# A two-layer decoder trunk on one core: where the conv taps stand among the attention score groups, and the order of the first weight's pieces

## The chip, the cores and the metric

The kernel runs on one core of a Trainium2 chip. The engines that matter are TensorE (PE in the profile, its weight loads PEld), VectorE (DVE), ScalarE (ACT), GpSimd (POOL) and SyncE (SP), which issues most DMAs. The metric is the time of one execution in device microseconds; lower is better. The time given for a kernel is the median of several runs.

## The reference

A trunk of two layers works on 512 tokens of width 1024 in float32. Cut to what matters here:

```python
for l in range(DEPTH):                                    # 2 layers
    h = x + 0.5 * swiglu(rms_norm(x, ffn1_norm[l]), w1, w3, w2)      # width 2816
    n = rms_norm(h, mix_norm[l])
    u_conv, q, k, v, q_mem = jnp.split(n @ w_in[l], splits, axis=-1)
    y_conv = conv_module(u_conv, ...)     # GLU, causal depthwise conv of 31 taps, 384 channels, LayerNorm, swish
    y_swa  = sliding_window_attention(...)  # 6 q heads, 2 kv heads, window 128, learned sinks
    y_mem  = memory_attention(...)        # 4 heads over 256 memory tokens
    h = h + jnp.concatenate([y_conv, y_swa, y_mem], -1) @ w_out[l]
    h = h + 0.5 * swiglu(rms_norm(h, ffn2_norm[l]), w1b, w3b, w2b)
    x = rms_norm(h, final_norm[l])
```

Each depthwise tap multiplies 384 channels of a shifted sequence by one weight per channel and adds it to a running sum. The attention subtracts the maximum of each row of scores (with the sink, in the windowed kind) before the exponential.

## The kernel before, in words

**Data and matmuls.** Activations lie with the channels on the 128 partitions and the 512 tokens along the free axis. A float32 product is made of three matmuls of a reduced float format (`mm3`, L176 to L178): high by high, high by low, low by high. So each weight and each operand is split into a high and a low part. The split is a ScalarE copy (the high part) and a VectorE subtraction (the low part, L145 and L146), or, where VectorE is to be spared, two ScalarE copies and a GpSimd DMA that adds the weight from memory once more (`split_by_dma`, L150 to L152). Operands are split by `split_scaled` (L155, L156).

**A layer.** `ffn` runs the first feed-forward block in quarters of its 22 column tiles. The gate tiles from the fifth on come in pairs by a scheme with seven products for eight (`up_pair`). `mixer` then runs the steps that the string ORDER lists: conv projections (`c`), queries (`q`) and their transposes (`Q`), values (`v`) and theirs (`V`), the first two score groups (`g`), the attention (`a`), the conv taps (`t`) and the swish with its LayerNorm (`s`). At the end the output projection's conv rows are added, and the second feed-forward block follows.

**Score groups.** `attention` walks through ten groups of (block, head pair). `begin(n)` puts the scores of group n into PSUM (`scored`, L763 and L769), VectorE takes their maxima (L773 or L788) and a bias (L774, or L789 and L790), ScalarE the exponentials (`powers`, L800), TensorE transposes them (`turned`, L810), ScalarE copies them (L812), TensorE multiplies by the values (`weighted`, L821), VectorE divides (`scaled`, L830 to L835), and `attended` transposes and splits the result (L844). Group n + 2 is begun while group n is worked on. The ScalarE exponential of the sink term (L829) needs a GpSimd sum (L791). The copies of the output weights' columns 0 to 3 (`out_weights`) stand in front of the loop and ahead of groups 3 and 5.

**Taps.** Three channel tiles of 31 taps make 93 VectorE operations a layer: one of L932 for each channel tile, and 30 of L939, each of which needs the one before it on the same channel tile. The first EARLY = 49 are free to start once their input is there. The other 44 are queued behind the biases of the ten groups, as many behind each as LATER says, with what is left over behind the last. In the program they come behind all of the attention.

**Swish.** GpSimd adds the three channel tiles (L945, L946), a matmul with ones gives the mean (L950), VectorE subtracts it (L953), ScalarE squares, and after the reciprocal root a spread over the partitions (`spread`, `kept`) gives the factor RL. Output rows of the attention parts (`out_rows`) are laid between these steps on TensorE.

**What sets the order.** The scheduler of the language orders each engine's instructions by a simulated timeline: the instruction that comes first in the program goes first among those that are ready. `tc.issue_after(x)` binds the block's instructions on x's engine to come behind x in that engine's order, and `queued()` does this with the last TensorE instruction. Every engine works its own list in order.

**Start.** SyncE loads the gains, then half of the first w1 tile, a chunk of x, half of the first w3 tile, and the other chunks of x with the second halves in the middle (L110 to L120).

Of the kernel before, what the change touches and what calls it, by code (L numbers as in the profile page):

```python
# [18 lines left out]
P = 128  # L19
# [45 lines left out]
def trunk(ctx: ExitStack, tc: tile.TileContext, xT, memT, pos, w1a, w3a, w2a, w1b, w3b, w2b,  # L65
# [44 lines left out]
    nc.sync.dma_start(gn, gains)  # L110
# [50 lines left out]
    def weights(src, cols, on, own=None):  # L161
        hi, lo = own or pair()
        if first:
            raw = first.pop(0)
            for c in halves:
                split(hi[:, c], lo[:, c], raw[:, c], V)
            return hi, lo
# [58 lines left out]
    class Stat:  # L226
# [5 lines left out]
        def square(self, out, src, scale):  # L232
            if self.on:
                self.on.tensor_tensor(out=out, in0=src, in1=src, op=ALU.mult)
            else:
                A.activation(out, src, AF.Square, scale=scale)
# [104 lines left out]
    def up_pair(l, w13, f, M):  # L341
# [26 lines left out]
        def add(out, a, b):  # L368
            V.tensor_tensor(out=out, in0=a, in1=b, op=ALU.add)  # L369
# [15 lines left out]
        for i in range(2):  # L385
# [4 lines left out]
            add(to[i][:, :, x1], zv[i].rearrange("p (n t) -> p n t", n=2), part[i][:, x0].unsqueeze(1).to_broadcast([P, 2, QT]))  # L390
# [14 lines left out]
    def ffn(l, w13, w2, x, sums, factors, last, at_product, aside=None):  # L405
# [138 lines left out]

    def head_scale(ps, col, n, out=None):

        sq = tm("hsq", "sq", 2)[:, 0 : n * HD]
        A.activation(sq, ps, AF.Square, scale=col)
# [74 lines left out]
    def mixer(l, x, st, last):  # L623
# [113 lines left out]

        def value_columns(t):
# [12 lines left out]
        sinks, nsinks = by_half(sink), by_half(nsink[:, l, :])  # L751

        def scored(kind, pairs):
# [17 lines left out]
            if not masked:  # L771
                for i in range(2):
                    V.tensor_reduce(out=nmr[:, b, i], in_=pp[i], axis=AX.X, op=ALU.max)  # L773
                biased[len(biased)] = V.scalar_tensor_tensor(out=nmr[:, b], in0=nmr[:, b], scalar=-1.0, in1=by_half(rm[:, b, :]),  # L774
                                                             op0=ALU.mult, op1=ALU.mult)
# [11 lines left out]
            for i in range(2):  # L787
                V.tensor_reduce(out=each(nmw, i), in_=pp[i], axis=AX.X, op=ALU.max)  # L788
            V.scalar_tensor_tensor(out=at_(nmw), in0=at_(nmw), scalar=-1.0, in1=rr, op0=ALU.mult, op1=ALU.mult)  # L789
            biased[len(biased)] = V.tensor_tensor(out=at_(nmw), in0=at_(nmw), in1=per(nsinks), op=ALU.min)  # L790
# [32 lines left out]
        def scaled(kind, b, po):  # L823
# [3 lines left out]
            if kind == "w":  # L827
                e = esw[:, b]
                A.activation(e, e, AF.Exp)  # L829
# [31 lines left out]
        def attention():  # L861
# [69 lines left out]
        def taps(c):  # L931
            V.tensor_scalar(out=cv[:, c, :], in0=ypad[:, c, 0:S], scalar1=conv_w[:, c, 0:1], scalar2=conv_b[:, c : c + 1],  # L932
                            op0=ALU.mult, op1=ALU.add)
            for j in range(1, TAPS):

                n = c * TAPS + j - EARLY
                group = sum(n >= sum(LATER[:g]) for g in range(1, len(LATER)))
                with tc.issue_after(biased[group].ins) if n >= 0 else nullcontext():
# [184 lines left out]
```

## Time and profile before

| | |
|---|---|
| median of 3 runs | 1791.62 us (1790.84 to 1792.38) |
| profiled execution | 1790.99 us |
| its span, first to last instruction | 1789.2 us |
| mean granted TensorE clock | 0.994 |
| HBM read, written | 249.40 MB, 2.10 MB |
| mean DMA rate | 142 GB/s |

The profile gives the busy time of each engine, and the trace every instruction with the idle time of its engine before it and what ended that time. Times are microseconds from the start of the span. The granted clock is the share of full speed that TensorE was given in a stretch. A row of the table of windows gives a stretch, its length, the busy time of each engine with the number of instructions, the granted clock, the share of the DMA engines and their rate. A row of the timeline gives start and length, engine, line, operation, what is written and read, and in brackets the idle time before it with what ended it.

### The profile page before, as it was taken

The numbers are of one execution on the slowest core, as the hardware profiler recorded it, in microseconds if no ns is written. First come the engines' busy times: TensorE is split into PE (matmuls) and PEld (weight loads), VectorE is DVE, ScalarE is ACT, GpSimd is POOL, SyncE is SP. The second block draws the span as 40 slices with busy tenths as digits, with TensorE's granted clock in tenths as the row PEclk, the third lists the DMA queues.
The fourth block names the chain that finished last, engine by engine and source line by source line (L and its number), as shares of the span: only waits on it lengthen the run. The fifth ranks groups of instructions, "written<-read, shape, count | busy, mean of one in ns | idle before, by whom it ended". The sixth has DMA issues, their size and how long they took to land.

```text
span 1789.2 us, 28081 instructions
## 1 busy us (share of the span) xinstructions
PE 1757.0 (98%) x11004; PEld 1581.5 (88%) x11004; DVE 1272.3 (71%) x1887; ACT 899.4 (50%) x1367; POOL 194.4 (11%) x217
## 2 busy tenths in 40 slices
PE   8999999999999999999999999999999999999997
PEld 6989999878788989898889898989787889998986
DVE  6969666589947857575678685756797567666755
ACT  6646444464765535353655453535455655453532
POOL 1001000034221000000010000000441210000000
PEclk9999999999999999999999999999999999999998
DMA  9456555183167547464656474643631966574622
GB/s 280 125 163 177 165 139 145 57 217 70 30 176 172 139 136 177 127 173 128 165 136 170 131 190 135 169 114 105 158 70 30 234 127 171 136 183 119 168 74 82
DMA packets 95892, 253.32 MB, mean 142 GB/s; under 512 B 9872, under 2 KB 14224, under 8 KB 95760
## 3 DMA queue, kind: packets, MB, share of 16 engines
q1 hardware_dynamic: 77040, 190.45, 34.9%
q0 software_dynamic: 18720, 61.09, 19.3%
q8 instruction: 86, 1.41, 0.3%
q14 instruction: 46, 0.38, 0.1%
HBM read 249.40 MB, written 2.10 MB: 141 GB/s over the span
## 4 chain that ended last, share of the span: by engine, by line
PE 81%; issue 6%; DVE 6%; DMA 4%; ACT 3%; POOL 0%; SPq 0%; POOLq 0%; DVEq 0%; ACTq 0%
PE mm L177 12%; PE mm L176 11%; PE mm L178 11%; PE po L176 8%; PE po L178 8%; PE po L177 8%; PE pt L176 6%; PE pt L177 6%; PE pt L178 6%; DVE there L939 2%; DMA glo<-in_wqk 1%; DMA raw<-in_wout 1%; DVE wlo L146 1%; PE cf L178 1%; PE cf L176 1%
## 5 line engine op out<-in xcount | busy, mean ns | idle before, releaser
L145 ACT ACTIVATE whi<-raw 128x1024 fp32r<-128x1024 f32 (+3 forms) x344 | 324.5, 945 | 440.5 <-PE mm L177 223.5
L146 DVE TENSOR_TENSOR wlo<-raw,whi 128x1024 fp32r<-128x1024 f32 (+3 forms) x344 | 372.0, 1083 | 133.9 <-ACT whi L145 132.6
L177 PE MATMUL mm<-glo,whi 128*128 128x512 f32 x752 | 293.3, 390 | 0.8 <-DVE glo L146 0.8
L176 PE MATMUL mm<-ghi,whi 128*128 128x512 f32 x752 | 293.3, 392 | 0.0
L178 PE MATMUL mm<-ghi,wlo 128*128 128x512 f32 x734 | 285.7, 389 | 0.9 <-DVE wlo L146 0.9
L177 PE MATMUL po<-ml,whi 128*128 128x256 f32 x864 | 244.5, 283 | 0.0
L178 PE MATMUL po<-mh,wlo 128*128 128x256 f32 x864 | 244.5, 283 | 0.0
L176 PE MATMUL po<-mh,whi 128*128 128x256 f32 x864 | 244.4, 283 | 0.0
L176 PE MATMUL pt<-xhi,whi 128*128 128x256 f32 x864 | 243.3, 283 | 0.6 <-DVE g L369 0.6
L178 PE MATMUL pt<-xhi,wlo 128*128 128x256 f32 x864 | 243.9, 283 | 0.0
L177 PE MATMUL pt<-xlo,whi 128*128 128x256 f32 x864 | 243.9, 283 | 0.0
L475 DVE SCALAR_TENSOR_TENSOR h<-mm,h 128x512 f32<-128x512 f32 x128 | 87.8, 689 | 133.3 <-PE mm L178 133.3
L177 PEld LDWEIGHTS mm<-glo,whi 128*128 128x128 f32 x752 | 141.3, 188 | 29.9 <-DVE glo L146 1.6
L176 PEld LDWEIGHTS mm<-ghi,whi 128*128 128x128 f32 x752 | 141.3, 188 | 29.4 <-DVE h L475 1.2
L176 PEld LDWEIGHTS pt<-xhi,whi 128*128 128x128 f32 x864 | 165.2, 192 | 1.7 <-DVE g L369 0.8
L177 PEld LDWEIGHTS pt<-xlo,whi 128*128 128x128 f32 x864 | 165.7, 192 | 0.8
L176 PEld LDWEIGHTS po<-mh,whi 128*128 128x128 f32 x864 | 165.8, 192 | 0.7
L177 PEld LDWEIGHTS po<-ml,whi 128*128 128x128 f32 x864 | 165.8, 192 | 0.6
L178 PEld LDWEIGHTS po<-mh,wlo 128*128 128x128 f32 x864 | 165.8, 192 | 0.0
L178 PEld LDWEIGHTS pt<-xhi,wlo 128*128 128x128 f32 x864 | 165.6, 192 | 0.0
L178 PEld LDWEIGHTS mm<-ghi,wlo 128*128 128x128 f32 x734 | 137.8, 188 | 30.2 <-DVE wlo L146 1.3
L939 DVE SCALAR_TENSOR_TENSOR there<-ypad,par,there 128x512 f32<-128x512 f32 x180 | 136.7, 770 | 1.6
(312 smaller groups left out, 3312.9 us busy)
## 6 DMA issues: line engine op xcount, KB each, us to landing
raw<-in_w2a SPq DMA_DIRECT2D x48, 384.0 KB, 3.5
raw<-in_w2b SPq DMA_DIRECT2D x48, 384.0 KB, 3.6
raw<-in_w1b SPq DMA_DIRECT2D x26, 512.0 KB, 3.7
raw<-in_w3b SPq DMA_DIRECT2D x26, 512.0 KB, 4.1
raw<-in_w1a SPq DMA_DIRECT2D x25, 512.0 KB, 3.7
raw<-in_w3a SPq DMA_DIRECT2D x25, 512.0 KB, 3.8
wsum<-in_w1a SPq DMA_DIRECT2D x18, 512.0 KB, 4.5
wsum<-in_w3a SPq DMA_DIRECT2D x18, 512.0 KB, 4.4
```

The source lines that it names most:

```text
L145: A.activation(hi, x, AF.Copy)
L146: on.tensor_tensor(out=lo, in0=x, in1=hi.bitcast(F32), op=ALU.subtract)
L176: T.matmul(ps, a[0], b[0], start=first, stop=False, **more)
L177: T.matmul(ps, a[0], b[1], start=False, stop=False, **more)
L178: tail[0] = T.matmul(ps, a[1], b[0], start=False, stop=last, **more)
L475: added = V.scalar_tensor_tensor(out=h[:, d, :], in0=ps, scalar=0.5, in1=h[:, d, :], op0=ALU.mult, op1=ALU.add)
L939: V.scalar_tensor_tensor(out=cv[:, c, :], in0=ypad[:, c, j : j + S], scalar=conv_w[:, c, j : j + 1], in1=cv[:, c, :], op0=ALU.mult, op1=AL ...
```

## The change

The change has seven parts.

1. Start: the first w1 tile comes in three pieces (256, 256 and 512 columns); the first quarter is loaded ahead of the gains, the second before the second chunk of x.
2. ORDER puts the values of block 2 (`v2`) ahead of `V1`, and the taps (`t`) ahead of the first score group. EARLY is 55. Each score group lays its own taps behind its bias, by the new LATER: 0, 8, 4, 3, 2, 1, 1, 1, 1 and 17. From the second group on, the maxima are queued behind the taps laid so far. The order of taps is: channel tile 0, 24 of tile 1, 17 of tile 2, then seven pairs that alternate between tiles 1 and 2, then the last seven of tile 2.
3. The exponential of the sink term goes behind the last exponential of its block. The output weights' columns 0 to 2 are split in the values of block 0, column 3 in those of block 2.
4. The second to fourth tile of the query weights are split behind the last square of the mixer's operand.
5. RL is copied by VectorE; the last pair of the conv output weights is copied behind the last swish.
6. The scaling of h by the block-output norm in layer 1 is done in two halves behind two successive pairs.
7. Helpers return the instructions that the others are bound to.

```diff
-ORDER = "c00 c01 q0 c10 q1 c11 Q0 q2 q3 Q1 c20 c21 Q2 v0 v1 V0 Q3 V1 g0 g1 v2 v3 a t0 t1 t2 s"
-EARLY = 49
-LATER = (1, 12, 5, 4, 3, 3, 3, 3, 3, 3)
+ORDER = "c00 c01 q0 c10 q1 c11 Q0 q2 q3 Q1 c20 c21 Q2 v0 v1 V0 Q3 v2 V1 t g0 g1 v3 a s"
+EARLY = 55
+LATER = (0, 8, 4, 3, 2, 1, 1, 1, 1, 17)
...
-    nc.sync.dma_start(gn, gains)
...
+    pieces = [slice(0, 256), slice(256, 512), slice(512, UNIT)]
     for k in range(KD):
-        if k % 4 == 0:
-            nc.sync.dma_start(first[0][:, halves[k // 4]], w1a[0, 0, :, halves[k // 4]])
+        if k in (0, 1, 4):
+            c = pieces[min(k, 2)]
+            nc.sync.dma_start(first[0][:, c], w1a[0, 0, :, c])
+        if not k:
+            nc.sync.dma_start(gn, gains)
...
-                    if f == PLAIN:
-                        with tc.issue_after(M.gated.ins):
-                            after()
+                    if f in (PLAIN, PLAIN + 2):
+                        with tc.issue_after((M.gated if f == PLAIN else M.turned).ins):
+                            after(f > PLAIN)
...
-                ww["q"] = [weights(wqk[l, i], 1024, G if i else V, spare()) for i in range(4)]
+                ww["q"] = []
+                for i in range(4):
+                    with tc.issue_after(operand.stats[0][0].done.ins) if i else nullcontext():
+                        ww["q"].append(weights(wqk[l, i], 1024, G if i else V, spare()))
...
+            for d in {0: (0, 1, 2), 2: (3,)}.get(t, ()):
+                with tc.issue_after((squared[-1] if d > 1 else keyed[2]).ins):
+                    out_weights(d)
...
+        to_do = [(c, j) for c in range(2) for j in range(TAPS)][:EARLY]
+        to_do += [(2, j) for j in range(TAPS - 14)]
+        for j in range(14):
+            to_do += [(1, j) for j in range(j + EARLY - TAPS, TAPS)][:1] if j + EARLY < 2 * TAPS else []
+            to_do.append((2, TAPS - 14 + j))
+        tapped = []
+
+        def taps(n=EARLY):
+            for c, j in [to_do.pop(0) for _ in range(n)]:
...
+        def between():
+            return tc.issue_after(tapped[-1].ins) if biased else nullcontext()
+
+        def taps_behind(small):
+            with tc.issue_after(small.ins):
+                taps(LATER[len(biased)])
+            biased[len(biased)] = small
...
-            for i in range(2):
-                V.tensor_reduce(out=each(nmw, i), in_=pp[i], axis=AX.X, op=ALU.max)
+            with between():
+                for i in range(2):
+                    V.tensor_reduce(out=each(nmw, i), in_=pp[i], axis=AX.X, op=ALU.max)
...
-                A.activation(e, e, AF.Exp)
+                with tc.issue_after(raised[kind, b, CC - 1].ins):
+                    A.activation(e, e, AF.Exp)
...
-            for d in range(2):
-                with tc.issue_after(keyed[2].ins):
-                    out_weights(d)
...
-                if n in (3, 5):
-                    with tc.issue_after(raised[GROUPS[n - 1][0], *GROUPS[n - 1][-1]].ins):
-                        out_weights(len(out_w))
...
-                RL = kept(spread(r), "RL")
+                RL = kept(spread(r), "RL", V)
...
-            A.activation(own[0], raw[:, 0 : 2 * CCH], AF.Copy)
-            A.activation(own[1], raw[:, 0 : 2 * CCH], AF.Copy, scale=-1.0)
+            with tc.issue_after(silus[0].ins) if i == 3 else nullcontext():
+                A.activation(own[0], raw[:, 0 : 2 * CCH], AF.Copy)
+                A.activation(own[1], raw[:, 0 : 2 * CCH], AF.Copy, scale=-1.0)
...
-                    for d in range(KD):
+                    for d in range(4 * half, 4 * half + 4):
```

More of the change, by code (lines that the diff above doesn't have):

```diff
@@ L164, in weights @@
             raw = first.pop(0)
-            for c in halves:
+            for c in halves if not first else pieces:
                 split(hi[:, c], lo[:, c], raw[:, c], V)
@@ L235, in square @@
             else:
[L236 removed]
+                self.done = A.activation(out, src, AF.Square, scale=scale)
         def add(self, src, scale=1.0, last=False):
@@ L368, in add @@
         def add(out, a, b):
-            V.tensor_tensor(out=out, in0=a, in1=b, op=ALU.add)
+            return V.tensor_tensor(out=out, in0=a, in1=b, op=ALU.add)
         for i in range(2):
@@ L621, in prepare, with mixer @@
         memory(l)
-    def mixer(l, x, st, last):
+    def mixer(l, operand, st, last):
+        x = operand.x
         o = CC * TAPS
@@ L786, in scored @@
                 rr = by_half(rq[:, b, 0:NH])[:, :, c : c + n]
-            for i in range(2):
-                V.tensor_reduce(out=each(nmw, i), in_=pp[i], axis=AX.X, op=ALU.max)
+            with between():
+                for i in range(2):
+                    V.tensor_reduce(out=each(nmw, i), in_=pp[i], axis=AX.X, op=ALU.max)
             V.scalar_tensor_tensor(out=at_(nmw), in0=at_(nmw), scalar=-1.0, in1=rr, op0=ALU.mult, op1=ALU.mult)
-            biased[len(biased)] = V.tensor_tensor(out=at_(nmw), in0=at_(nmw), in1=per(nsinks), op=ALU.min)
+            small = V.tensor_tensor(out=at_(nmw), in0=at_(nmw), in1=per(nsinks), op=ALU.min)
+            taps_behind(small)
             G.tensor_tensor(out=at_(esw), in0=at_(nmw), in1=per(sinks), op=ALU.add)
@@ L928, in out_rows @@
                     mm3(oo[d], at(out_w[d], ALL, blk(n)), y[CC + n], n == CC, False)
[L931 to L938, printed above, removed]
-                    V.scalar_tensor_tensor(out=cv[:, c, :], in0=ypad[:, c, j : j + S], scalar=conv_w[:, c, j : j + 1],
-                                           in1=cv[:, c, :], op0=ALU.mult, op1=ALU.add)
+        silus = []
         def swish():
@@ L1006, in factors @@
         def factors(r):
-            return gain, kept(spread(r), "R"), lambda: None
+            return gain, kept(spread(r), "R"), lambda half: None
         return lambda: rms_cols(st, D), factors
@@ L1027, in trunk @@
         before, st = st, Stat("st")
-        mixer(l, nxt.x, before, into(gn[:, l, N_FFN2], (st, None)))
+        mixer(l, nxt, before, into(gn[:, l, N_FFN2], (st, None)))
         sums, factors = stages(st, gn[:, l, N_FFN2])
```

29 lines of the change are left out of this document (20 added, 9 removed).

## The prediction

> **What bounds the kernel now.** I read the page first, for the engine that fills the span.
>
> ```profile
> span 1789.2 us, 28081 instructions
> ...
> PE 1757.0 (98%) x11004; PEld 1581.5 (88%) x11004; DVE 1272.3 (71%) x1887; ACT 899.4 (50%) x1367; POOL 194.4 (11%) x217
> ...
> L939 DVE SCALAR_TENSOR_TENSOR there<-ypad,par,there 128x512 f32<-128x512 f32 x180 | 136.7, 770 | 1.6
> ```
>
> TensorE is busy in 98% of the span, and the change removes none of its matmuls. It can only win back time in which TensorE waits or runs at a reduced clock: 1789.2 - 1757.0 = 32 us of waits plus the slow stretches. The profiled execution took 1790.99 us, 1.8 us more than its span; the median of the three runs is 1791.62 us. I work out differences on the profiled one and subtract them from the median.
>
> Next I cut the span into stages by the table of windows, to see where TensorE is not full. The scores groups of the mixer stand out. The first row below holds the score groups of layer 0 from the third group's bias to the last one's; the other two are the slowest stretches of the two layers. Columns: PE, PEld, DVE, ACT, POOL busy, then the granted clock.
>
> ```profile
> 454.10:486.80 32.70, 29.74 (x226) 24.34 (x226) 31.00 (x71) 25.17 (x59) 6.76 (x9) 0.95 0.22 41
> ...
> 459.00:465.00 6.00, 6.00 (x37) 4.46 (x37) 4.96 (x12) 3.50 (x10) 1.49 (x2) 0.72 0.62 109
> ...
> 1342.00:1348.00 6.00, 6.00 (x26) 4.53 (x26) 3.29 (x7) 2.68 (x7) 1.49 (x2) 0.50 0.60 109
> ```
>
> VectorE is busy for 31.00 of 32.70 us there: in this stage it, not TensorE, is nearly full. TensorE is idle for 2.96 us, and later runs at 0.72 of its clock for 6 us (6 x 0.28 = 1.7 us lost) and in layer 1 at 0.50 (6 x 0.50 = 3.0 us lost). The same windows for the tap line alone:
>
> ```profile
> 454.10:486.80 32.70, 17.89 (x24) 0.95 0.22 41
> 486.80:494.00 7.20, 5.21 (x7) 1.00 0.01 2
> ```
>
> 24 taps stand between those two biases and 7 behind the last, as LATER says (5+4+3+3+3+3+3, and 3 plus the 4 that are left). One costs 17.89/24 = 0.745 us of VectorE. TensorE's own waits around there:
>
> ```profile
> 438.04 0.44 PE L581 MATMUL pt<-cst,aux 128*128 128x128 f32 x2 [0.81 <-ACT there L583]
> ...
> 458.71 1.11 PE L821 MATMUL po<-mvn,aux 128*128 128x65 f32 x8 [1.83 <-ACT aux L812]
> ```
>
> The 1.83 us wait is ScalarE's queue: its exp of the sink term waits for GpSimd, and a w_out copy stands ahead of the probabilities' copy that TensorE needs.
>
> ```profile
> 456.64 0.21 ACT L829 ACTIVATE esw<-esw 128x6 f32<-128x6 f32 x1 [0.94 <-POOL esw L791]
> 456.76 0.79 ACT L800 ACTIVATE uu<-mm,nmw,rq 128x128 f32<-128x128 f32 x2
> 457.44 0.73 ACT L150 ACTIVATE whi<-raw 128x640 fp32r<-128x640 f32 x1
> 458.07 0.59 ACT L812 ACTIVATE aux<-pt 128x512 f32<-128x512 f32 x1
> ```
>
> **The change, part by part.** *Score groups.* Behind the biases of groups 2 to 8 the new LATER puts 4+3+2+1+1+1+1 = 13 taps instead of 24: 11 x 0.745 = 8.2 us of VectorE leave this stretch. Six more taps run before the groups (55 for 49); the values of block 2, moved ahead of them, give VectorE that time. Moving those 24 matmuls between Q3 and V1 also covers the 0.81 us wait at 438.04. The exp of the sink term goes behind the last exp of its block, and the w_out copies of columns 2 and 3 go to the values stage, so both rows ahead of 458.07 leave that place. What TensorE can win at most is what it loses: 2.96 idle + 0.81 + the clock, 1.7 or 3.0, that is 5.5 us in layer 0 and 6.8 in layer 1. It cannot win all: groups still pass from ScalarE to TensorE to VectorE and back. I take nine tenths, **5.0 and 6.0 us**. Bounds: 1.5 us a layer if only the ScalarE reordering counts, 9 if VectorE's 8.2 us all turn into time beside the 0.81.
>
> *The tail.* Ten taps more stand behind the last group's bias (17 for 7). Who waits: the GpSimd sum over the channel tiles, then the mean's matmul at L950, and behind that matmul, in TensorE's order, all that is left of the output rows.
>
> ```profile
> 491.87 1.53 DVE L939 SCALAR_TENSOR_TENSOR there<-ypad,par,there 128x512 f32<-128x512 f32 x2
> ...
> 493.54 1.29 POOL L946 TENSOR_TENSOR aux<-aux,there 128x512 f32<-128x512 f32 x1 [5.96 <-DVE there L939]
> ...
> 500.52 1.02 PE L950 MATMUL pt<-aux,onesq 128*128 128x512 f32 x2
> ```
>
> The sum is ready at 493.54 + 1.29 = 494.83, and TensorE comes for it at 500.52: a slack of 5.7 us. Ten taps add 7.45 us. GpSimd's other sum (L945, channel tiles 0 and 1) now also falls among the last taps, because tile 1 ends there, and such a neighbour doubles a tap:
>
> ```profile
> 454.73 1.27 POOL L945 TENSOR_TENSOR aux<-there 128x512 f32<-128x512 f32 x1
> ...
> 455.08 1.47 DVE L939 SCALAR_TENSOR_TENSOR there<-ypad,par,there 128x512 f32<-128x512 f32 x1
> ```
>
> That is 1.47 - 0.745 = 0.7 more, 8.2 in all, less 5.7 of slack: TensorE waits **2.5 us a layer**. Bounds: 0, if TensorE's remaining score work behind the bias stretches instead; 5.5, if the clock then drops as in the row of 1342 (3.0). I keep the clock out of the sum here, since the matmuls before this wait are dense.
>
> The Trainium skill, TensorE: Matmul & The Clock Gate, section "HAM oscillation", asks for no idle gaps of TensorE above some 3.4 us; a wait of 2.5 us would keep the clock. The trace does not quite agree: the 1.83 us gap at 458.71 is followed by a clock of 0.72.
>
> *Behind the tail.* The spread of the LayerNorm scale (RL) is copied by VectorE, and the fourth w_out copy pair goes behind the swish. Today the copy queues behind that pair, which waits for a DMA:
>
> ```profile
> 517.69 0.85 ACT L987 ACTIVATE whi<-raw 128x768 fp32r<-128x768 f32 x1 [3.02 <-DMA raw<-in_wout]
> 518.44 0.83 ACT L988 ACTIVATE whi<-raw 128x768 fp32r<-128x768 f32 x1
> 519.17 0.58 ACT L221 ACTIVATE RL<-pt 128x512 f32<-128x512 f32 x1
> ```
> ```profile
> 527.31 0.50 PE L177 MATMUL mm<-glo,whi 128*128 128x512 f32 x1 [0.28 <-DVE glo L146]
> ```
>
> All but 0.28 us of that is hidden behind output rows; with the restart I take **0.4 us a layer** as gain (0 to 1). The moved pair's GpSimd DMAs feed the last two columns, 54 matmuls later, and stay hidden.
>
> *Queries.* Three copy pairs of w_qk go behind the last square of the normalised operand. Today they stand ahead of its last chunk, and TensorE waits; but the last w_qk transfer lands just in time:
>
> ```profile
> 373.88 0.50 PE L176 MATMUL mm<-xhi,whi 128*128 128x512 f32 x1 [0.46 <-ACT xhi L155]
> ...
> 387.28 0.50 PE L177 MATMUL mm<-glo,xhi 128*128 128x512 f32 x1 [0.17 <-DMA glo<-in_wqk]
> ```
> ```profile
> 374.26 1.04 ACT L150 ACTIVATE ghi<-raw 128x1024 fp32r<-128x1024 f32 x1
> ```
> ```profile
> 376.54 10.70 DMA glo<-in_wqk
> ```
>
> A copy costs 1.04 us, three pairs 6.2. The third pair starts at 374.26, right behind the last square, and two pairs (4.2 us) stand ahead of that square now. VectorE makes the last chunk of h late too, so I let the square end half of 4.2 earlier, at 372.2. Then the third pair ends, and the third transfer starts, at 378.4 instead of 376.54. It lands between 376.54 + 10.70 = 387.24, if the bandwidth that the transfers share sets its end, and 1.9 us later. The buffers of the next conv weights come free later too; they are needed only behind that wait. The landing decides, so the 0.46 gained mostly vanishes in it: **0.5 us lost a layer**, between 0.6 gained and 1.9 lost.
>
> *Block-output norm.* Eight scalings of h block VectorE in one piece before layer 1's first quarter ends; now four go behind each of two pairs.
>
> ```profile
> 967.47 5.38 DVE L1053 SCALAR_TENSOR_TENSOR h<-h,gn,RL 128x512 f32<-128x512 f32 x8
> ```
> ```profile
> 976.11 0.50 PE L178 MATMUL mm<-ghi,wlo 128*128 128x512 f32 x1 [0.89 <-DVE wlo L146]
> ```
>
> Half the block removes 2.7 us ahead of a 0.89 us wait: **0.9 us gained**, once (0 if the second half makes a wait of its own).
>
> *Start.* The first quarter of w1 comes ahead of the gains. The first matmul may start a few tenths earlier, but the second operand chunk sets the pace, and from there VectorE has no gap:
>
> ```profile
> 2.59 5.60 DMA h<-in_xT
> ```
> ```profile
> 8.97 0.75 DVE L156 SCALAR_TENSOR_TENSOR xlo<-h,gn,xhi 128x512 fp32r<-128x512 f32 x1 [0.95 <-ACT xhi L155]
> ```
>
> It lands at 8.19 behind the same number of bytes as before, so **0** (0.4 either way, for one more issue and smaller pieces).
>
> **Sum.** -5.0 - 6.0 + 2 x 2.5 - 2 x 0.4 + 2 x 0.5 - 0.9 = -6.7 us: 1791.62 - 6.7 = 1784.9 us.
>
> **The rivals.** *The tail is free.* If the groups end so much earlier that the taps run while TensorE still has transposes, the 5.0 us come back and the w_qk landing does not slip (-1.0): 1778.9 us. For it: from the bias at 486.80 to L950 at 500.52 TensorE has 13.7 us of its own, and seventeen taps take 17 x 0.745 = 12.7. Against: VectorE has the last groups' small operations in that time too, and the GpSimd sum comes on top.
>
> *The clock stays low.* The gap of 1.83 us may not be what slows TensorE; thin work around it may be. Then 1.7 + 3.0 us are not won: 1789.6 us. For it: between 454.10 and 486.80 the stage is a chain of short matmuls, which the change leaves as they are. The Trainium skill's rule of 3.4 us, named above, speaks for this one: a shorter gap should not have lowered the clock.
>
> *The seventeen taps hold up the last groups.* This ends slower. Until now the taps stand behind all attention work in the order of the program and only fill gaps. Now they stand ahead of what the last groups still need from VectorE (a reciprocal, a scaling, the splits of four transposes). Ten of the seventeen alternate between two channel tiles, so none waits for the one just before it, and the scheduler may issue them in one row. Then those small operations come up to 7.45 us later. TensorE, which needs the splits for its transposes, waits about 6.5 of these and starts again at a low clock (1.7 and 3.0). The layers change by -5.0 + 6.5 + 1.7 = +3.2 and -6.0 + 6.5 + 3.0 = +3.5; with the other parts' -0.7: 1797.6 us. It decides once the small operations wait longer than what the groups have won, 5 to 6 us. Against: the other seven taps of the row are one chain, and chained taps leave room between them.
>
> **How the numbers follow.** A measurement of this kernel can tell some 0.2%, 3.6 us, from no change: below 1788.0 is faster, above 1795.2 slower. The forecast has 0.47, the free tail 0.18, the clock that stays low 0.22, the taps that hold up the groups 0.13. Faster: nine tenths of the forecast, the free tail, a little of the low clock, 0.62. Same: the rest of the forecast and most of the low clock, 0.22. Slower: the last rival and the w_qk landing at its worst (twice 1.9) with a low clock, 0.16. The range goes from 1777 (free tail, a little more won in the groups) to 1795 (low clock, and the w_qk transfer or the tail at its bound).
>
> **What would show it.** Right: 13 taps between the third and the last bias, that stretch 4 to 6 us shorter, no wait near 1.8 us behind the third group, the granted clock of the two slow windows near 1; a wait of 1 to 4 us ahead of L950's matmul; the wait at 976 gone; first operand chunks without a wait, and a longer wait for the w_qk transfer. Wrong: VectorE still full between the biases with TensorE idle, or waits of the last groups' transposes on VectorE's splits of several microseconds, or a clock of 0.5 to 0.7 with the gap gone.

## The result, and the profile after

The changed kernel takes **1801.16 us** (median of 4 runs, 1799.62 to 1804.4), the kernel before, run beside it, 1791.23 us: ratio 1.0057, 95% interval 1.0040 to 1.0075. It is slower, and it lies above the range forecast. The profiled execution took 1800.05 us; its page begins:

```profile
span 1798.3 us, 28085 instructions
...
PE 1763.1 (98%) x11004; PEld 1586.3 (88%) x11004; DVE 1275.9 (71%) x1890; ACT 899.5 (50%) x1366; POOL 191.5 (11%) x217
```

The span grew by 9.1 us. I cut both timelines at the same instructions: the last addition to h in the first FFN, the first transposes of probabilities (L810, now L855), the last scores matmul (L769, now L811), the mean's matmul (L950, now L980), the last addition to h in the mixer. Times are in us; the difference and the forecast add both layers. The forecast's 11.0 for the groups also holds what it hoped for from the 0.81 us wait, which lies in the stretch before them.

| stretch | before, layers 0 and 1 | after | difference | forecast |
|---|---|---|---|---|
| start to the last h of the first FFN | 370.42 | 369.95 | -0.5 | 0 |
| to the first transposes of probabilities (conv, queries, values) | 78.37, 78.87 | 82.09, 84.52 | **+9.4** | +1.0 |
| to the last scores (the groups) | 35.42, 37.11 | 31.90, 31.90 | **-8.7** | -11.0 |
| to the mean's matmul (the tail) | 16.31, 16.29 | 21.25, 21.27 | **+9.9** | +5.0 |
| to the last h of the mixer | 42.41, 42.59 | 43.06, 43.56 | +1.6 | -0.8 |
| second FFN, first FFN of layer 1 | 709.64 | 708.07 | -1.6 | -0.9 |
| last FFN | 361.81 | 360.73 | -1.1 | 0 |

**The groups** did what was hoped. The first row lies between the third and the last bias. The next two are the windows that were slow before; the same work comes 3 us later in layer 0 and 9 us later in layer 1 now, and the clock is 1.00 there too. Columns are as in the prediction. The taps of the first window stand behind them:

```profile
457.87:485.87 28.00, 27.56 (x223) 23.02 (x223) 23.95 (x60) 22.79 (x54) 3.21 (x5) 1.00 0.00 1
459.00:465.00 6.00, 5.79 (x47) 4.81 (x47) 5.86 (x13) 4.80 (x14) 0.64 (x1) 1.00 0.00 0
1342.00:1348.00 6.00, 6.00 (x51) 4.95 (x51) 5.55 (x14) 4.47 (x11) 2.14 (x2) 1.00 0.01 3
```
```profile
457.87:485.87 28.00, 9.73 (x14) 1.00 0.00 1
```

28.0 us for 32.7, TensorE idle for 0.44 instead of 2.96, the clock at 1.00 where it was 0.72 and 0.50, about thirteen taps (14 records touch the window) for 24. The wait of 1.83 us has shrunk to 0.21.

**The queries** lost it first. TensorE's waits of layer 0, from the timeline:

```profile
386.08 0.50 PE L180 MATMUL mm<-glo,xhi 128*128 128x512 f32 x1 [1.75 <-DMA glo<-in_wqk]
389.89 0.50 PE L180 MATMUL mm<-glo,xhi 128*128 128x512 f32 x1 [2.16 <-DMA glo<-in_wqk]
```

and of layer 1, where matmuls at about half the clock follow (0.62 and 0.80 us instead of 0.50; the granted clock from 1273 to 1278 is 0.56):

```profile
1273.35 0.62 PE L180 MATMUL mm<-glo,xhi 128*128 128x512 f32 x1 [2.17 <-DMA glo<-in_wqk]
1277.16 0.80 PE L180 MATMUL mm<-glo,xhi 128*128 128x512 f32 x1 [1.05 <-DMA glo<-in_wqk]
```

The three GpSimd transfers of w_qk (start of the issue first), in the kernel before and in the changed one, with the times to landing of the latter. In layer 0 of the changed kernel TensorE waits for the second and the third:

```profile
370.45 0.86 POOL L152 DMA_DIRECT2D glo<-in_wqk  x1 [32.45 <-ACT glo L151]
373.51 0.86 POOL L152 DMA_DIRECT2D glo<-in_wqk  x1 [2.21 <-PE mm L178]
```
```profile
374.11 0.86 POOL L155 DMA_DIRECT2D glo<-in_wqk  x1 [36.58 <-ACT glo L154]
376.22 0.90 POOL L155 DMA_DIRECT2D glo<-in_wqk  x1
377.89 0.87 POOL L155 DMA_DIRECT2D glo<-in_wqk  x1 [0.78 <-ACT glo L154]
...
DMA to landing us min/median/max: 7.4/9.8/12.0
```

They start 3.7, 2.7 and 1.4 us later, and land 2.5, 3.1 and 2.6 us later (381.50, 386.04, 389.85), while TensorE comes 1.4 us earlier.

A smaller loss sits behind them: the second score group now waits for the columns that V1 has just copied, 1.43 us in each layer, where the 0.81 us wait stood.

```profile
446.70 0.48 PE L811 MATMUL mm<-mT,there 64*128 64x256 f32 x1 [1.43 <-ACT there L588]
```

**The tail** lost it a second time. TensorE's waits there, VectorE's row of seven taps with the last block's reciprocal and scaling behind it, GpSimd's sum, and the clock in the two layers:

```profile
490.89 0.44 PE L890 MATMUL pt<-cst,aux 128*128 128x128 f32 x2 [1.27 <-DVE glo L149]
491.88 1.11 PE L855 MATMUL pt<-cst,uu 128*128 128x128 f32 x4 [0.55 <-DVE glo L149]
501.40 0.52 PE L890 MATMUL pt<-cst,aux 128*128 128x128 f32 x3 [1.08 <-DVE aux L881]
505.18 1.02 PE L980 MATMUL pt<-aux,onesq 128*128 128x512 f32 x2
```
```profile
493.40 6.37 DVE L781 SCALAR_TENSOR_TENSOR there<-ypad,par,there 128x512 f32<-128x512 f32 x7
499.69 0.16 DVE L876 TENSOR_TENSOR rd<-po,esw 128x6 f32<-128x6 f32 x1
...
500.70 0.56 DVE L881 TENSOR_TENSOR aux<-po,rd 128x384 f32<-128x384 f32 x1
```
```profile
500.70 1.27 POOL L976 TENSOR_TENSOR aux<-aux,there 128x512 f32<-128x512 f32 x1 [6.21 <-DVE rd L877]
```
```profile
490.00:500.00 10.00, 8.55 (x34) 7.45 (x34) 9.79 (x17) 1.02 (x3) 1.27 (x1) 0.66 0.01 2
1380.00:1390.00 10.00, 8.19 (x34) 6.62 (x32) 9.75 (x16) 0.98 (x2) 1.77 (x2) 0.69 0.00 0
```

The mean's matmul itself waits for nothing: the sum is ready at 501.97. TensorE is late because the splits (glo) and the last scaling come late from a VectorE that is 98% busy, and because its clock falls to 0.66 and 0.69. The windows from the last scores to the mean's matmul, layers 0 and 1 before and then after, tell the two apart:

```profile
484.21:500.52 16.31, 14.51 (x97) 12.40 (x94) 10.72 (x27) 6.68 (x18) 1.92 (x2) 1.00 0.00 1
1368.54:1384.83 16.29, 14.48 (x98) 12.41 (x95) 10.72 (x27) 6.68 (x18) 1.92 (x2) 1.00 0.01 2
```
```profile
483.93:505.18 21.25, 17.98 (x97) 15.19 (x94) 17.57 (x35) 6.58 (x18) 3.17 (x3) 0.84 0.00 1
1372.72:1394.00 21.28, 17.64 (x98) 14.64 (x94) 17.58 (x35) 6.58 (x18) 3.17 (x3) 0.84 0.00 1
```

TensorE's idle time (length less busy time) grew from 1.80 and 1.81 us to 3.27 and 3.64. Its busy time for the same matmuls grew by 3.5 and 3.2 us, with the clock at 0.84. So about two thirds of the tail's loss is the clock, and one third waits.

### The profile page after: what moved, and what is told of

It is laid out like the page before. It is cut to its first block, busy times and chain, and to the rows that moved or that the text cites. A ratio compares the mean times of both kernels' runs of the same rounds, so it can differ in the third digit from the quotient of the medians.

```text
span 1798.3 us, 28085 instructions
## 1 busy us (share of the span) xinstructions
PE 1763.1 (98%) x11004; PEld 1586.3 (88%) x11004; DVE 1275.9 (71%) x1890; ACT 899.5 (50%) x1366; POOL 191.5 (11%) x217
## 4 chain that ended last, share of the span: by engine, by line
PE 86%; issue 5%; DVE 3%; DMA 3%; ACT 2%; POOL 0%; SPq 0%; POOLq 0%; DVEq 0%; ACTq 0%
PE mm L180 12%; PE mm L179 12%; PE mm L181 12%; PE po L179 9%; PE po L181 9%; PE po L180 9%; PE pt L179 6%; PE pt L181 6%; PE pt L180 6%; DMA glo<-in_wqk 1%; DVE there L781 1%; PE po L866 1%; PE mm L811 1%; PE cf L179 1%; PE cf L180 1%
## 5 line engine op out<-in xcount | busy, mean ns | idle before, releaser
L148 ACT ACTIVATE whi<-raw 128x1024 fp32r<-128x1024 f32 (+4 forms) x345 | 324.5, 943 | 445.5 <-PE mm L180 225.4
L149 DVE TENSOR_TENSOR wlo<-raw,whi 128x1024 fp32r<-128x1024 f32 (+4 forms) x345 | 371.8, 1079 | 138.5 <-ACT whi L148 137.4
```

Of the source, the lines that this page charges most:

```text
L148: A.activation(hi, x, AF.Copy)
L149: on.tensor_tensor(out=lo, in0=x, in1=hi.bitcast(F32), op=ALU.subtract)
```

## The experiments

Theory A: the loss is the late w_qk transfers (7 to 8 us in both layers) and the taps behind the last bias (5 us a layer), which together outweigh what the groups win. Its rivals are named with each run: that the queries' loss would appear elsewhere anyway (D), that ScalarE's new order and not the taps made the groups faster (C), that in the tail the amount of VectorE's work counts and not its order (B). Ratios are to the kernel before as timed in the same round (medians 1790.45 to 1791.89), with the 95% interval; groups and tail are the stretches of the table above, in layers 0 and 1.

| kernel | median us | ratio | groups | tail |
|---|---|---|---|---|
| before | 1791.23 | | 35.42, 37.11 | 16.31, 16.29 |
| the changed kernel | 1801.16 | 1.0057 (1.0040 to 1.0075) | 31.90, 31.90 | 21.25, 21.27 |
| 1 changed, queries as before | 1794.42 | 1.0015 (1.0006 to 1.0024) | 31.90, 31.91 | 20.51, 20.25 |
| 2 before, queries' part alone | 1797.69 | 1.0039 (1.0027 to 1.0051) | 35.38, 35.36 | 16.27, 16.26 |
| 3 changed, only the third w_qk pair held | 1792.70 | 1.0014 (1.0004 to 1.0024) | 31.91, 31.91 | 20.47, 21.86 |
| 4 changed, 7 taps behind the last bias | 1798.87 | 1.0046 (1.0033 to 1.0059) | 33.33, 33.34 | 17.24, 21.21 |
| 5 before, ScalarE's part alone | 1787.95 | 0.9981 (0.9972 to 0.9989) | 33.56, 33.56 | 16.32, 16.34 |
| 6 changed, last scaling ahead of 8 taps | 1810.08 | 1.0111 (1.0098 to 1.0124) | 31.91, 31.90 | 24.46, 24.12 |
| 7 changed, memory scaling ahead of 17 taps | 1807.70 | 1.0091 (1.0078 to 1.0104) | 31.91, 32.28 | 23.65, 22.17 |
| 8 run 5, with start and split norm | 1784.84 | 0.9969 (0.9957 to 0.9980) | 33.56, 33.57 | 16.33, 16.34 |
| 9 run 8, 18 taps behind the last bias | 1790.99 | 0.9999 (0.9991 to 1.0008) | 31.81, 31.81 | 19.48, 19.48 |
| 10 run 8, 13 taps behind the last bias | 1784.40 | 0.9963 (0.9951 to 0.9975) | 32.12, 32.12 | 17.22, 17.24 |
| 11 changed, three losing places mended | 1788.18 | 0.9987 (0.9979 to 0.9996) | 33.53, 33.54 | 17.24, 17.27 |
| 12 changed, swish part undone | 1803.61 | 1.0067 (1.0051 to 1.0084) | 31.91, 31.91 | 21.27, 21.25 |

**1. The changed kernel with the queries as before.**

```
-                ww["q"] = []
-                for i in range(4):
-                    with tc.issue_after(operand.stats[0][0].done.ins) if i else nullcontext():
-                        ww["q"].append(weights(wqk[l, i], 1024, G if i else V, spare()))
+                ww["q"] = [weights(wqk[l, i], 1024, G if i else V, spare()) for i in range(4)]
```

> The changed kernel, but the w_qk copies stand again where they stood before the change (not behind the last square). Theory A (the w_qk transfers that start 1.4 to 3.7 us later are the largest single loss: net 3.1 us in layer 0 and 4.5 in layer 1, read from the two traces): the first wait on the second w_qk transfer (1.75 us) goes, the third wait (2.16) shrinks to 0.2, the 0.46 wait on the operand's last chunk comes back, and the time falls from 1801.2 by 7 to 8 us to about 1793.6. Rival D (the queries are only slow because the next conv weights load beside them, or because work that was late anyway is waited for one stage further on): the waits move to the next stage and the time stays within 2 us of 1801.

Measured 1794.42 us. From 1.0057 to 1.0015 is 0.42%, 7.5 us: A holds for the queries, D falls.

**2. The kernel before with the queries' part alone** (the reverse of that edit, put into the kernel before).

> The kernel before, with only the queries' part of the change (three w_qk copy pairs behind the last square). Theory A: 3.1 and 4.5 us lost in the two layers, 1791.2 becomes about 1798.8. Rival D: within 2 us of 1791. If the loss needs the rest of the change beside it (its conv loads, its ScalarE order), the two runs of the queries' part, on and off, will not agree.

Measured 1797.69 us, 0.39% or 7.0 us. Off and on agree, so the loss needs nothing else of the change. Its waits in layer 0 are like those of the changed kernel in layer 1:

```profile
387.82 0.59 PE L177 MATMUL mm<-glo,xhi 128*128 128x512 f32 x1 [1.94 <-DMA glo<-in_wqk]
391.62 0.80 PE L177 MATMUL mm<-glo,xhi 128*128 128x512 f32 x1 [1.08 <-DMA glo<-in_wqk]
```

**3. Only the third pair held.**

```
-                    with tc.issue_after(operand.stats[0][0].done.ins) if i else nullcontext():
+                    with tc.issue_after(operand.stats[0][0].done.ins) if i == 3 else nullcontext():
```

> The changed kernel, but only the third w_qk copy pair is held behind the last square; the first two go as before the change. My prediction reckoned with the third transfer's own start alone and took the shared bandwidth as a floor at 387.24. Seven transfers of 512 KB (three of w_qk, four of conv) follow one another from 370.45 on in the kernel before and from 373.83 on in the changed one, and land 2.5 to 3.1 us later. Theory S (the shared stream sets the landings, and its start is what the change moved): with the first two started at 370.5 and 373.6 again, the third lands within 1 us of 387.2 though it starts later, the waits of 1.75 and 2.16 shrink to under 1 in sum, and the time falls by 5 us or more, to 1794 to 1796. Rival (each transfer's own start sets its landing): the third lands at 376.5 + 10.7 + the delay of its copy, 389 to 390, its wait stays near 2 us and only the second's 1.75 goes: 1798.

Measured 1792.70 us, 0.43% less than the changed kernel and a little below the range of theory S, and no wait for w_qk is left in layer 0. The GpSimd issues of this run, and the time to landing:

```profile
369.91 0.86 POOL L155 DMA_DIRECT2D glo<-in_wqk  x1 [32.33 <-ACT glo L154]
373.10 0.86 POOL L155 DMA_DIRECT2D glo<-in_wqk  x1 [2.33 <-PE mm L181]
376.13 0.86 POOL L155 DMA_DIRECT2D glo<-in_wqk  x1 [2.17 <-ACT glo L154]
...
DMA to landing us min/median/max: 8.0/8.7/10.5
```

The condition on the third pair alone moves nothing, because that pair comes behind the last square anyway (376.13, for 376.54 in the kernel before). All of the loss is in holding the first two. This also means that the third's own start was not moved alone here, so the run doesn't strictly separate the shared stream from each transfer's own start. The stream is favoured by the changed kernel's own rows: its third transfer starts 1.35 us later, yet lands 2.6 later, because it takes 11.96 us instead of 10.70.

**4. Seven taps behind the last bias again.**

```
-LATER = (0, 8, 4, 3, 2, 1, 1, 1, 1, 17)
+LATER = (0, 8, 4, 4, 3, 3, 3, 3, 3, 7)
```

> The changed kernel with LATER = 0,8,4,4,3,3,3,3,3,7: seven taps behind the last group's bias as before the change, ten moved back between the groups; everything else of the change kept. Two theories of the gain of 3.5 and 5.2 us between the first turned transposes and the last scores. A (fewer taps between the groups make it): the stretch grows back to 35.4 and 37.1 us and the tail gives back its 4.9 us a layer, so the time is 1801.2 + 8.7 - 9.9 = about 1800. C (ScalarE's order makes it: the sink term's exp and the w_out copies out of the groups): the stretch stays at 32 to 33 us, the tail still gives back 4.9 a layer, and the time falls to about 1791 to 1793.

Measured 1798.87 us, nearer to A's 1800. But the stretches show both theories half right: the groups went back by 1.4 us only (33.33), so ten taps fewer between the biases are worth 1.4 us a layer, not 3.5 and 5.2. The tail gave back 4.0 us in layer 0 and nothing in layer 1. There the same instructions ran at a lower clock, down to 0.52 between 1380 and 1390 (windows from the last scores to the mean's matmul, layers 0 and 1):

```profile
487.19:504.43 17.24, 14.68 (x98) 12.38 (x94) 11.65 (x27) 6.59 (x18) 3.19 (x3) 1.00 0.00 1
1374.74:1395.95 21.21, 19.12 (x98) 16.36 (x95) 11.84 (x27) 6.70 (x18) 3.17 (x3) 0.76 0.01 1
```

**5. The kernel before with ScalarE's part alone.**

```
+                with tc.issue_after(raised[kind, b, CC - 1].ins):
                     A.activation(e, e, AF.Exp)          # the sink term
-            for d in range(2):
-                with tc.issue_after(keyed[2].ins):
-                    out_weights(d)
-                if n in (3, 5):
-                    with tc.issue_after(raised[GROUPS[n - 1][0], *GROUPS[n - 1][-1]].ins):
-                        out_weights(len(out_w))
+            for d in {0: (0, 1, 2), 2: (3,)}.get(t, ()):         # in values(t)
+                with tc.issue_after((squared[-1] if d > 1 else keyed[2]).ins):
+                    out_weights(d)
```

> The kernel before, with only ScalarE's part of the change: the exp of the sink term behind the last exp of its block, the w_out copies 0 to 2 in the values of block 0 and copy 3 in those of block 2. Taps as before. C: most of 3.5 and 5.2 us is won, 1791.2 becomes 1783 to 1785, the 1.83 us wait at 458.71 is gone and the clock stays near 1 in the groups. A (the taps make the gain): under 2 us won, 1789 to 1791; the wait of 1.83 shrinks but VectorE, busy 31.0 of 32.7 us there, puts its own waits in its place.

Measured 1787.95 us, 0.19% faster, between what C and A expected. The groups went from 35.42 and 37.11 to 33.56 in both layers: 1.9 and 3.6 us. In layer 1 that is two thirds of what the whole change won, in layer 0 half. Part of the 3.6 is the luck of one execution: in run 2, whose groups are those of the kernel before, layer 1 took 35.36 us at a clock of 0.95, for 37.11 at 0.91. The window after the 1.83 us wait now has the full clock, and VectorE gets more done in it (5.93 and 5.96 us of 6, for 4.96 and 3.29):

```profile
459.00:465.00 6.00, 5.77 (x45) 4.34 (x43) 5.93 (x13) 3.73 (x9) 0.64 (x1) 1.00 0.00 0
1342.00:1348.00 6.00, 5.77 (x42) 3.97 (x40) 5.96 (x16) 4.52 (x11) 1.29 (x2) 1.00 0.00 0
```

**6. The last block's scaling ahead of eight of the seventeen taps.** The other nine stay where they were.

```
+            with tc.issue_after(weighed["w", 3].ins):    # L881 of the last block
+                taps(8)
             out_rows(1, MEMORY)
```

> The changed kernel; of the 17 taps behind the last bias nine stay where they are and eight wait for the scaling of the last block (L881), which in the changed kernel is issued behind sixteen of them. VectorE's order is the same up to that scaling. Theory A (order: the taps hold up the last block's scaling, so TensorE comes to the mean 4.95 us late whatever else it waits for): the scaling moves from 500.70 to about 495, TensorE loses its 1.08 us wait for it and is no longer held behind it, and about 2.5 to 3 us a layer come back: 1801 becomes 1795 to 1796. Rival B (the amount: seventeen taps behind the last bias fill VectorE until the mean, in any order): the wait moves from the scaling to the mean's matmul, which then waits 2 us or more for GpSimd's sum, and the time stays within 1.5 us of 1801.

Measured 1810.08 us, 0.54% slower than the changed kernel; neither theory foresaw that. VectorE's and TensorE's timelines say why:

```profile
498.89 0.17 DVE L878 TENSOR_TENSOR rd<-po,esw 128x6 f32<-128x6 f32 x1 [5.39 <-PE po L866]
```
```profile
508.40 1.74 PE L984 MATMUL pt<-aux,onesq 128*128 128x512 f32 x2 [4.37 <-POOL aux L980]
```

The scaling's input comes only at 498.9, so VectorE stood idle for 5.39 us and the mean's matmul came 3.2 us later than in the changed kernel. My expectation took the wrong weighted matmuls for its input.

**7. The seventeen taps behind the scaling of the last memory block.**

```
+                    with tc.issue_after(weighed["r", 3].ins):
+                        taps(LATER[-1])               # instead of behind the last bias
```

> The changed kernel; the 17 taps behind the last bias all wait for the scaling of the last memory block (L881, at 490.09 behind six taps in the changed kernel). The run that held eight taps back for the very last scaling told nothing of the order, since that one's input comes only at 498.9. Theory A (order): without taps ahead of it the scaling comes at about 487, TensorE's waits of 1.27 and 0.55 us and the half clock behind them go, and the mean's matmul comes 2.5 us or more earlier than in the changed kernel, 21.2 us behind the last scores: 5 us for the two layers, about 1796. Theory B (amount): VectorE has seventeen taps (12.7 us) and 4.2 us of small operations from the last bias at 485.94 on, GpSimd's sum takes 1.27 more, so the mean can't come before 504.1, 20.2 us behind the last scores: the waits move to the mean's matmul, which waits 3 us or more for GpSimd, and at most 1 us a layer is won, 1799 to 1801.

Measured 1807.70 us. A (order) falls: the memory block's scaling now starts 4.0 us behind the last scores instead of 6.2, and the tail isn't won back. (The last block's scaling still stands behind nine taps here.) B named the right thing, the amount, but neither the price nor the place: VectorE waits between the small operations instead of filling the gaps with taps, so the tail grows from 21.25 to 23.65 and 22.17, and the wait is not the mean's but that of the last block's transposes for their scaling:

```profile
504.00 0.85 PE L893 MATMUL pt<-cst,aux 128*128 128x128 f32 x3 [3.66 <-DVE aux L884]
```

My reading of runs 6 and 7 together: with this many taps in the tail, a gap left open on VectorE comes back as time.

**8. ScalarE's part, the start and the split norm.** The diff is run 5's and the two hunks of the change (first quarter of w1, and the block-output norm in two halves).

> The kernel before with ScalarE's part of the change (which alone gave 1788), the start (first quarter of w1 in front) and the split block-output norm; taps, order of the mixer and queries as before. My prediction put the start at 0 and the split at -0.9. If they hold: about 1787.0; the first matmul at 5.6 instead of 6.3 us and no 0.89 us wait at 976. If the start's earlier first matmul is also kept (0.5 us by the two traces): 1786.5. A rival for which both are swallowed by a later wait: 1788.

Measured **1784.84 us**, ratio 0.9969: 0.31% faster than the kernel before, 1.7 us below the lowest figure expected, and 0.12 points below run 5, whose interval it overlaps. The wait at 976 is gone: TensorE is idle for 0.00 us from 960 to 990 in every run with the split that I cut there and for 0.89 or 0.90 in those without. The first matmul starts at 5.48 (5.97 in run 5).

**9. The taps' part alone, on run 8.**

```
-LATER = (1, 12, 5, 4, 3, 3, 3, 3, 3, 3)
+LATER = (1, 12, 4, 3, 2, 1, 1, 1, 1, 1)
```

> The fastest kernel so far (the one before with ScalarE's part, the start and the split: 1784.8), and in it LATER = 1,12,4,3,2,1,1,1,1,1: thirteen taps between the third and the last bias as in the changed kernel, the other eleven behind the last bias, eighteen in all there; the order of the tiles and of the program as before the change. It is the taps' part alone. By the sums so far the groups win 1.4 us a layer (33.5 to about 32) and the tail loses 3.7 to 5: 1784.8 becomes 1789 to 1792. If the taps' part had been good and was only spoilt by its neighbours in the change: 1782.

Measured 1790.99 us, 0.30% slower than run 8. The groups win 1.75 us a layer and the tail loses 3.15, at a clock of 1.00. For both layers that is 2.8 us of the 0.30%, 5.4 us; the rest was not traced. Here, where the taps stand behind the attention in the program's order, the wait of the forecast appears in TensorE's timeline, at the size of the forecast:

```profile
500.30 1.12 PE L954 MATMUL pt<-aux,onesq 128*128 128x512 f32 x2 [2.67 <-POOL aux L950]
```

**10. Thirteen taps behind the last bias, on run 8.**

```
-LATER = (1, 12, 5, 4, 3, 3, 3, 3, 3, 3)
+LATER = (1, 12, 4, 3, 3, 2, 2, 2, 2, 2)
```

> The fastest kernel so far with LATER = 1,12,4,3,3,2,2,2,2,2: six of its taps moved behind the last bias (13 there, for 7 in the fastest and 18 in the run that moved eleven). Slack theory: in the fastest kernel GpSimd's sum ends at 494.20 and TensorE comes to the mean at 499.85, so 5.65 us are free; six taps are 4.5 us and fit, the mean doesn't wait, and the groups win 6/11 of the 1.75 us that eleven taps gave, 0.95 a layer: 1784.8 becomes about 1783. Rival (small operations: taps behind the last bias hold up the last groups' reciprocals, scalings and splits from the first moved tap on, and the loss grows with each): stretch from the last scores to the mean longer than 16.3 us by 1.5 or more, no gain, 1785 to 1788.

Measured 1784.40 us (0.9963); against run 8 nothing can be told apart. The groups win 1.44 us a layer, the tail loses 0.9. The mean doesn't wait, as the slack theory has it (GpSimd's and TensorE's timelines):

```profile
496.96 1.29 POOL L950 TENSOR_TENSOR aux<-aux,there 128x512 f32<-128x512 f32 x1 [10.85 <-PE pt L854]
```
```profile
500.11 1.02 PE L954 MATMUL pt<-aux,onesq 128*128 128x512 f32 x2
```

But 0.94 us appears at the last scaling, as the rival has it, at less than its price. Both kernels, 8 and 10, beat the kernel before.

**11. The changed kernel with its three losing places mended**: runs 1 and 4, and

```
-ORDER = "... v0 v1 V0 Q3 v2 V1 t g0 g1 v3 a s"
+ORDER = "... v0 v1 V0 v2 V1 t g0 Q3 g1 v3 a s"
```

> The changed kernel with its three losing places undone: w_qk copies as before; LATER = 0,8,4,4,3,3,3,3,3,7; and the order V0 v2 V1 t g0 Q3 g1 v3, so that the last key transposes (Q3) stand between V1 and the second group, which waited 1.43 us for V1's copies. If the losses add up as read from the single runs: after_spread's 1798.9, less 7 for the queries, less 0.7 and 1.1 for the 1.43 us wait: about 1790. ScalarE's order, the split and the start are still in it, so it should be no slower than the kernel before; and if VectorE's total work is what holds the whole mixer (it is 89 to 99% busy from 390 to 490 us), it can't fall below the run with ScalarE's part alone, 1788.

Measured 1788.18 us, 2 us better than expected and faster than the kernel before, yet 0.18% above run 8 (the two intervals just touch). The 1.43 us wait shrinks to 0.84 in layer 0. What the change's taps ahead of the attention and its order bring beyond ScalarE's part, the start and the split is a loss, or at best nothing.

**12. The swish part undone** (the scale copied by ScalarE, no condition on the fourth w_out pair).

> The changed kernel with the LayerNorm scale copied by ScalarE again and the fourth w_out pair not held behind the swish. My prediction had 0.4 us a layer gained by that part. If it gains: 1802. If it gains nothing, because ScalarE waits for the next weights' DMA ahead of the swish (4.62 us at 524.20): 1801. If holding ScalarE's queue behind that DMA costs (the Silu came at 522.02 before and at 526.58 after, with the mean 4.7 us later): 1800 or below.

Measured 1803.61 us, ratio 1.0067, above all three figures expected; its interval overlaps that of the changed kernel. So this part neither gains nor costs what can be told. In the changed kernel ScalarE waits ahead of the swish for something else, by its timeline:

```profile
524.20 1.06 ACT L148 ACTIVATE whi<-raw 128x1024 fp32r<-128x1024 f32 x1 [4.62 <-DMA raw<-in_w1b]
```

## Why the prediction was wrong, step by step

- **Queries: the step that failed most.** Forecast 0.5 us lost a layer, at worst 1.9; the runs show 7.0 to 7.7 us for both. I followed one transfer, the third, and took its earlier landing (387.24) as a floor set by the shared bandwidth. But the first transfer moved from 370.45 to 374.11 and the second from 373.51 to 376.22, and the second and third landed at 386.04 and 389.85, the latter beyond my bound of 389.1. Whether a later start of the shared stream did this or each transfer's own start was not separated. I priced the delay of the third pair, which the condition on it alone does not cause (run 3), and not that of the first two. Nor did I ask about the second transfer, which alone makes a wait of 1.75 us, or charge TensorE's earlier arrival against the landing.
- **Tail: mis-sized, and by another mechanism.** Forecast 2.5 us a layer, bounds 0 and 5.5; measured 4.95. The mean's matmul was to wait for the sum; instead the last groups' splits and the last scaling came late and the clock fell. The step that failed is "I keep the clock out of the sum here, since the matmuls before this wait are dense": the waits grew by 1.5 and 1.8 us only, less than my 2.5, but the clock at 0.84 cost 3.5 and 3.2 us. That is the mechanism of my third rival (0.13), smaller than its price of 6.5 and a low clock. Without the interleaved order of tiles and program (run 9) the forecast's own wait came, 2.67 us. Why the clock falls in the changed kernel's tail and not in run 9's was not settled.
- **Score groups: right in place, a little too large.** Forecast 5.0 and 6.0, of which some 0.7 a layer was for the 0.81 us wait ahead of them; measured 3.5 and 5.2, inside the bounds of 1.5 to 9. Of the 5.2, 1.75 us is a lower clock in layer 1 of the kernel before's trace (0.91), which run 2 (0.95) did not have. The clock came back and the gap went, so the rival of a clock that stays low falls. Runs 4, 5 and 9 share the gain out: ScalarE's order 1.9 and 3.6, eleven taps 1.75. Taps worth 8.2 us of VectorE gave 1.75 us. With ScalarE's part in, TensorE was idle for only 1.72 of the 33.56 us at a clock of 1.00 (run 5), so little was left to win: VectorE's busy time was not TensorE's loss. Moving them was a bad bargain, since behind the last bias they cost 3.15.
- **Between the queries and the groups.** I gave the block-2 values between Q3 and V1 credit for the 0.81 us wait and did not ask who needs V1 next: the second group, which now waits 1.43 us. The stretch from the queries' end to the first transposes grew by 0.7 and 1.1 us by the timelines.
- **Behind the tail**: 0.4 us a layer forecast; no gain (run 12). The 1.6 us that this stretch grew in the profile is not explained; it ranges from 42.4 to 45.2 us over all runs.
- **Split norm: right.** 0.9 forecast, 0.89 measured, by the wait's own row. **Start**: 0 forecast within 0.4. The first matmul comes 0.7 us earlier, but no gain can be told at the end of the first FFN: that point lies between 369.85 and 371.64 in the traces with the new start and between 370.42 and 371.49 in those without.

The queries' term was out by 6.0 to 6.7 us (7.0 to 7.7 for 1.0) and the tail's by 4.9. By these figures, with both as forecast, the 9.1 us of loss would have been a gain of about 2. In both I had followed a single item to the end of its path.

## What to carry to other kernels

Here a condition that delayed the first loads of a stream delayed every landing in it: price each transfer that TensorE will ask for, against the time at which it will ask. Before work is moved off a full engine, compare what it is worth there (here 0.16 us of a tap's 0.745) with the slack where it goes (5.65 us ahead of the mean in run 8, some seven taps), and with every other wait there: in run 10 six taps fit into that slack and still cost 0.9 us at the last scaling. Parts of one change are best run alone: here three of them made 1784.84 us, and the others cost more than these won.

## What the runs showed of the hardware

**The clock can fall with short waits alone.** In run 4 both layers issue the same instructions. TensorE's longest waits in the tail are, in the two layers,

```profile
495.63 0.66 PE L855 MATMUL pt<-cst,uu 128*128 128x128 f32 x4 [0.96 <-DVE glo L149]
...
1378.08 0.66 PE L855 MATMUL pt<-cst,pr 128*128 128x128 f32 x4 [0.67 <-DVE glo L149]
```

yet the granted clock is 1.00 in the one tail and 0.76 in the other, which take 17.24 and 21.21 us. The length of a single wait doesn't decide it. The Trainium skill, TensorE: Matmul & The Clock Gate, section "HAM oscillation", asks for no idle gaps above some 3.4 us; by it none of these would have slowed the clock, and the trace doesn't agree. The drop also differs from one kernel's trace to the next where TensorE's idle time is the same: between 900 and 960 us, where it is idle for some 0.25 us in each, the clock is 1.00 in the changed kernel and in run 4, and 0.97 in runs 1, 3, 7 and 11. The stretch of the second FFN and the first FFN of layer 1 takes 708.1 us in the former two and 709.4 to 709.7 us in the latter four.

**Accumulating transfers take long.** The 512 KB accumulating transfers of w_qk took 7.4 to 12.0 us beside the conv loads. The Trainium skill, DMA: Bandwidth & Descriptors, section "Anatomy of one DMA", gives a fit for one transfer issued by GpSimd from which I estimate 3.2 us. The trace doesn't agree, and the conv loads are not the whole reason: GpSimd's accumulating transfers of the same size in the feed-forward blocks of the kernel before took a median of 7.2 to 8.6 us, and SyncE's plain ones 3.7 to 4.5 (the last number of each row):

```profile
raw<-in_w1a SPq DMA_DIRECT2D x25, 512.0 KB, 3.7
wsum<-in_w1a POOLq DMA_DIRECT2D x18, 512.0 KB, 8.6
```
